# The second block's softmax: scaling by the reciprocal sums moved from a VectorE pass into the transposition on TensorE

## The chip, the cores and the metric

The kernel runs on one core of one Trainium2 chip. The metric is device time in microseconds (us), the median of several runs. A core has TensorE (PE, with its weight loads listed as PEld), VectorE (DVE), ScalarE (ACT), GpSimd (POOL) and the queues that issue transfers. A profile is one execution, recorded instruction by instruction.

## The reference

Two transformer blocks of different make, each of two layers, on 512 tokens of 1024 features, in fp32. The change touches the second block's two kinds of attention. In short:

```
# grouped-query attention: 8 query heads, 2 key heads, 512 keys
s = einsum('bqgrd,bkgd->bgrqk', qi, k) * scale
p = softmax(s, axis=-1)
o = einsum('bgrqk,bkgd->bqgrd', p, v)

# dilated attention: 4 heads, 3 groups of neighbours (steps 1, 4, 16)
s = einsum('bqhd,bqkhd->bhqk', qi, kg) * scale      # masked at the edges
lse = logsumexp(s); p = exp(s - lse)
out_g = einsum('bhqk,bqkhd->bqhd', p, vg)
o = sum over g of softmax over g of (lse_g) * out_g
```

The last line of the dilated attention is the same as one softmax over the keys of all three groups together, and so the kernel does it: 768 columns a query (512 of the first group, 128 each of the others), most of them masked.

## The kernel before

Activations lie with features on the partitions. Each projection is a set of TensorE products in which weights and activations are split in a high and a low part (`split`, `mm3`, lines 121 to 151): three products of 512 columns for each 128 features that are summed over. The weights are loaded, cast on ScalarE (L121) and their low part is made on GpSimd (L122).

`mixers2` runs once in each layer of the second block. It weaves generators: while `gqa` and then `dilated` yield between their steps, `dil_proj` and `gate` issue projections, so that on TensorE their products (L144, L145, L147) stand between the attention's own. A scheduler then fixes the order on each engine, and every engine works its own list in that order.

`gqa` goes over 4 pairs of heads (`u`) and 2 halves of the queries, 8 halves a layer. In a half, for two blocks of 128 queries (`b`) and two heads (`e`): scores in fp32 on TensorE (L1197, from `scores`; 128x512 each), their negated maximum on VectorE (L1221), exponentials with sums on ScalarE (L1225, tile `P`), the reciprocal of the sums (L1227) and a product of `P` with it, in place, both on VectorE (L1229). Then each 128x128 block of `P` is transposed on TensorE (L1237), four of them into one PSUM tile `pt` of two that rotate; ScalarE copies each filled `pt` to SBUF (L1239); the products with the values follow (L1245).

`dilated` does the same with one head at a time and 768 columns: scores L1197 (first pair of heads, 512 and twice 128 columns) or L1200 (second pair), mask and maximum L1268, exponentials L1273, reciprocal L1275, scaling L1276, transpositions L1284, copies L1286, products with the values L1292 and L1298. The first pair of heads runs among the projections of the second, the second among the gates.

A transposition has a block of `P` as its stationary operand and the identity as its moving one:

```
nc.tensor.transpose(pt[:, e, b], P[b][:, e, 128 * kb:128 * kb + 128], self.ident)
```

Of the kernel before, what the change touches and what calls it, by code (L numbers as in the profile page):

```python
# [14 lines left out]
ALU = mybir.AluOpType  # L15
# [74 lines left out]
class Kernel:  # L90
# [1111 lines left out]
    def head_gains(self):  # L1202
# [3 lines left out]
        q = self.hg.rearrange("p (l t g) -> p l t g", l=2, g=4)[:, :, :, 0:2]  # L1206
        nc.vector.tensor_scalar(out=q, in0=q, scalar1=0.125, scalar2=None, op0=ALU.mult)

    def gqa(self, q, k, V, outs):
        nc = self.nc  # L1210
        for u in range(4):
            t = self.new("of", [128, 512], "oa")
            for half in range(2):
                P = []
                for b in range(2):
                    Q = slice(256 * half + 128 * b, 256 * half + 128 * b + 128)
                    ps = self.psum("p2", [128, 2, 512])
                    for e in range(2):
                        self.scores(ps[:, e], q[u], k, e, Q, slice(0, 512))
                    nm = self.new("c1", [128, 2], "nm2")  # L1220
                    nc.vector.tensor_reduce(out=nm, in_=ps, axis=AX.X, op=ALU.max, negate=True)  # L1221
                    p = self.new("P", [128, 2, 512], "P2")
                    z = self.new("c1", [128, 2], "z2")
                    for e in range(2):
                        nc.scalar.activation(out=p[:, e], in_=ps[:, e], func=AF.Exp, bias=nm[:, e:e + 1], accum_out=z[:, e:e + 1])  # L1225
                    rz = self.new("c1", [128, 2], "rz2")
                    nc.vector.reciprocal(out=rz, in_=z)  # L1227
                    for e in range(2):
                        nc.vector.tensor_scalar(out=p[:, e], in0=p[:, e], scalar1=rz[:, e:e + 1], scalar2=None, op0=ALU.mult)  # L1229
                    P.append(p)  # L1230
                yield True
                PT = []
                for kb in range(4):
                    pt = self.psum("pt", [128, 2, 2, 128])
                    for e in range(2):
                        for b in range(2):
                            nc.tensor.transpose(pt[:, e, b], P[b][:, e, 128 * kb:128 * kb + 128], self.ident)  # L1237
                    w = self.new("W", [128, 2, 256], "PT2")
                    nc.scalar.copy(out=w, in_=pt.rearrange("p e b q -> p e (b q)"))  # L1239
                    PT.append(w)  # L1240
                yield True
                acc = self.psum("pt", [128, 256])
                for kb in range(4):
                    for e in range(2):
                        nc.tensor.matmul(acc[64 * e:64 * e + 64], V(0, kb)[:, 64 * e:64 * e + 64], PT[kb][:, e],  # L1245
                                         start=kb == 0, stop=kb == 3, tile_position=(0, 64 * e))
                nc.scalar.copy(out=t[:, 256 * half:256 * half + 256], in_=acc)
                yield True
            outs.append(t)

    def dilated(self, u, q, k, V, outs):

        nc = self.nc
        t = self.new("of", [128, 512], "ob")
        for half in range(2):
            PT = []
            for e in range(2):
                P = []
                for b in range(2):
                    r = 2 * half + b  # L1260
                    Q = slice(128 * r, 128 * r + 128)
                    ps = self.psum("p2", [128, 1024])
                    self.scores(ps[:, 0:512], q[0, u], k[0, u], e, Q, slice(0, 512))
                    for g in (1, 2):
                        self.scores(ps[:, 384 + 128 * g:512 + 128 * g], q[g, u], k[g, u], e, Q, Q)
                    p = self.new("P", [128, 768], "Pd")
                    mx = self.new("c1", [128, 1], "mx")
                    nc.vector.tensor_tensor_reduce(out=p, in0=ps[:, 0:768], in1=self.dmask[:, r], scale=1.0, scalar=-3e38,  # L1268
                                                   op0=ALU.add, op1=ALU.max, accum_out=mx)
                    nm = self.new("c1", [128, 1], "nmd")  # L1270
                    nc.vector.tensor_scalar(out=nm, in0=mx, scalar1=-1.0, scalar2=None, op0=ALU.mult)
                    z = self.new("c1", [128, 1], "zd")
                    nc.scalar.activation(out=p, in_=p, func=AF.Exp, bias=nm, accum_out=z)  # L1273
                    rz = self.new("c1", [128, 1], "rzd")
                    nc.vector.reciprocal(out=rz, in_=z)  # L1275
                    nc.vector.tensor_scalar(out=p, in0=p, scalar1=rz, scalar2=None, op0=ALU.mult)  # L1276
                    P.append(p)
                yield True
                for kp in range(3):
                    pt = self.psum("pt", [128, 2, 2, 128])  # L1280
                    for j in range(2):
                        for b in range(2):
                            c = 256 * kp + 128 * j
                            nc.tensor.transpose(pt[:, j, b], P[b][:, c:c + 128], self.ident)  # L1284
                    w = self.new("W", [128, 2, 256], "PTd")
                    nc.scalar.copy(out=w, in_=pt.rearrange("p j b q -> p j (b q)"))  # L1286
                    PT.append(w)
                yield True
            acc = self.psum("pt", [128, 256])
            for kb in range(4):  # L1290
                for e in range(2):
                    nc.tensor.matmul(acc[64 * e:64 * e + 64], V(1 + u, kb)[:, 64 * e:64 * e + 64], PT[3 * e + kb // 2][:, kb % 2],  # L1292
                                     start=kb == 0, stop=False, tile_position=(0, 64 * e))
            for g in (1, 2):
                for b in range(2):
                    B = slice(128 * b, 128 * b + 128)
                    for e in range(2):
                        nc.tensor.matmul(acc[64 * e:64 * e + 64, B], V(1 + 2 * g + u, 2 * half + b)[:, 64 * e:64 * e + 64],  # L1298
                                         PT[3 * e + 2][:, g - 1, B], start=False, stop=g == 2 and b == 1, tile_position=(0, 64 * e))
            nc.scalar.copy(out=t[:, 256 * half:256 * half + 256], in_=acc)  # L1300
            yield True
        outs.append(t)
# [423 lines left out]
```

## Time and profile before

| | |
|---|---|
| median of 3 runs | 3469.3 us (3465.06 to 3469.94) |
| the profiled execution's own time | 3459.91 us |
| its span, first to last instruction | 3458.1 us |
| mean granted TensorE clock | 0.981 |
| TensorE busy | 3302.1 us, 95% of the span |
| TensorE weight loads | 2627.1 us, 76% |
| VectorE busy | 1722.6 us, 50% |
| ScalarE busy | 1582.0 us, 46% |
| GpSimd busy | 1150.1 us, 33% |

The span is shorter than the time by what lies around the instructions. Busy shares are means over the whole program. Matmuls overlap, one starting before the one before it has ended, so a busy TensorE tells that it had something in flight, and the distance from start to start tells what an instruction costs in a row of its kind.

### The profile page before, as it was taken

The numbers are of one execution on the slowest core, as the hardware profiler recorded it, in microseconds if no ns is written. First come the engines' busy times: TensorE is split into PE (matmuls) and PEld (weight loads), VectorE is DVE, ScalarE is ACT, GpSimd is POOL, SyncE is SP. The second block draws the span as 40 slices with busy tenths as digits, with TensorE's granted clock in tenths as the row PEclk, the third lists the DMA queues.
The fourth block names the chain that finished last, engine by engine and source line by source line (L and its number), as shares of the span: only waits on it lengthen the run. The fifth ranks groups of instructions, "written<-read, shape, count | busy, mean of one in ns | idle before, by whom it ended". The sixth has DMA issues, their size and how long they took to land.

```text
span 3458.1 us, 47235 instructions
## 1 busy us (share of the span) xinstructions
PE 3302.1 (95%) x18518; PEld 2627.1 (76%) x18518; DVE 1722.6 (50%) x2736; ACT 1582.0 (46%) x2824; POOL 1150.1 (33%) x555
## 2 busy tenths in 40 slices
PE   6999998999998899989999999999999999999999
PEld 4666677888887666677888667888888767888887
DVE  5755468343345763564326965564315766462111
ACT  5555445242243554454333666543334666543333
POOL 1222033222235321234443312434444312444443
PEclk8999999999999899999999999999999999999999
DMA  7731134343334321145432101236422101222222
GB/s 275 261 107 55 44 102 142 106 137 113 110 120 156 110 79 42 45 166 191 164 116 102 60 32 58 95 122 211 154 93 91 67 31 54 84 95 90 95 96 97
DMA packets 146705, 377.87 MB, mean 109 GB/s; under 512 B 16737, under 2 KB 32690, under 8 KB 146354
## 3 DMA queue, kind: packets, MB, share of 16 engines
q1 hardware_dynamic: 146482, 374.85, 32.0%
q8 instruction: 146, 2.39, 0.3%
q14 instruction: 77, 0.63, 0.1%
HBM read 363.48 MB, written 9.86 MB: 108 GB/s over the span
## 4 chain that ended last, share of the span: by engine, by line
PE 58%; DVE 8%; ACT 2%; DMA 1%; issue 1%; POOL 0%; SPq 0%; DVEq 0%; ACTq 0%; POOLq 0%
PE pm L144 15%; PE pm L145 15%; PE pm L147 14%; PE p L1197 2%; DVE y L360 1%; DMA g<-in_w_mod 1%; PE pt L1245 1%; PE p L999 1%; PE pm L151 1%; PE pt L1237 1%; PE p L1200 1%; PE pt L145 1%; PE pt L144 1%; PE pt L1284 1%; PE pm L965 1%
## 5 line engine op out<-in xcount | busy, mean ns | idle before, releaser
L122 POOL TENSOR_TENSOR wlo<-raw,whi 128x1024 fp32r<-128x1024 f32 (+2 forms) x461 | 1090.7, 2367 | 2070.6 <-ACT whi L121 1942.8
L121 ACT CAST whi<-raw 128x1024 fp32r<-128x1024 f32 (+2 forms) x468 | 477.0, 1019 | 1065.2 <-PE pm L145 577.9
L144 PE MATMUL pm<-h,whi 128*128 128x512 f32 (+1 forms) x2312 | 855.8, 378 | 15.3 <-ACT raw_s L555 7.3
L145 PE MATMUL pm<-h,whi 128*128 128x512 f32 (+1 forms) x2312 | 842.8, 372 | 1.9 <-DVE h L388 1.9
L147 PE MATMUL pm<-h,wlo 128*128 128x512 f32 x1816 | 716.5, 395 | 2.6 <-POOL wlo L122 2.6
L144 PEld LDWEIGHTS pm<-h,whi 128*128 128x128 f32 x2312 | 441.8, 191 | 101.5 <-issue 10.1
L145 PEld LDWEIGHTS pm<-h,whi 128*128 128x128 f32 x2312 | 441.0, 191 | 78.4 <-issue 6.5
L144 PE MATMUL pm<-hid,whi 128*128 128x512 f32 (+1 forms) x1280 | 457.4, 367 | 4.0 <-DVE x L459 2.2
L145 PE MATMUL pm<-hid,whi 128*128 128x512 f32 (+1 forms) x1280 | 455.2, 365 | 2.9 <-DVE hid L527 2.9
L147 PEld LDWEIGHTS pm<-h,wlo 128*128 128x128 f32 x1816 | 343.3, 189 | 76.7 <-POOL wlo L122 4.3
L147 PE MATMUL pm<-hid,wlo 128*128 128x512 f32 x976 | 381.1, 390 | 0.2 <-POOL wlo L122 0.2
L527 DVE TENSOR_TENSOR hid<-relu,hid 128x512 fp32r<-128x512 f32 (+1 forms) x169 | 177.3, 1053 | 339.0 <-ACT hid L526 338.9
L273 DVE SCALAR_TENSOR_TENSOR p<-g,svec,p 128x512 f32<-128x512 f32 x280 | 211.2, 754 | 258.2 <-DMA g<-in_w_mod 255.3
L459 DVE SCALAR_TENSOR_TENSOR x<-pm,mod,x 128x512 f32<-128x512 f32 (+1 forms) x184 | 125.5, 684 | 383.0 <-PE pm L147 377.4
L144 PEld LDWEIGHTS pm<-hid,whi 128*128 128x128 f32 x1280 | 241.1, 188 | 46.9 <-issue 5.4
L145 PEld LDWEIGHTS pm<-hid,whi 128*128 128x128 f32 x1280 | 240.8, 188 | 41.5 <-DVE hid L527 3.5
L147 PEld LDWEIGHTS pm<-hid,wlo 128*128 128x128 f32 x976 | 183.6, 188 | 39.5 <-POOL wlo L122 1.4
L521 ACT ACTIVATE relu<-pm 128x512 f32<-128x512 f32 (+1 forms) x160 | 85.8, 536 | 130.2 <-PE pm L147 130.2
L978 ACT ACTIVATE D<-pt,cc 128x256 f32<-128x256 f32 (+1 forms) x176 | 72.8, 447 | 81.6 <-PE pt L972 43.3
L339 DVE TENSOR_TENSOR acc<-acc,sq 128x256 f32<-128x256 f32 (+1 forms) x96 | 89.0, 927 | 27.8 <-ACT sq L331 26.3
L523 ACT ACTIVATE relu<-relu 128x512 f32<-128x512 f32 (+1 forms) x169 | 96.3, 570 | 4.8
L387 ACT ACTIVATE h<-y,mod 128x256 fp32r<-128x256 f32 (+1 forms) x136 | 67.0, 527 | 60.1 <-DVE y L360 59.3
(418 smaller groups left out, 4791.3 us busy)
## 6 DMA issues: line engine op xcount, KB each, us to landing
g<-in_w_mod SPq DMA_DIRECT2D x352, 256.0 KB, 3.3
raw<-in_w_in SPq DMA_DIRECT2D x142, 512.0 KB, 3.5
raw<-in_w_down SPq DMA_DIRECT2D x136, 512.0 KB, 3.5
raw<-in_w_up SPq DMA_DIRECT2D x128, 512.0 KB, 3.5
raw<-in_w_out SPq DMA_DIRECT2D x24, 512.0 KB, 3.5
g<-in_w_mod SPq DMA_DIRECT2D x16, 512.0 KB, 7.1
raw<-in_w_out SPq DMA_DIRECT2D x16, 384.0 KB, 3.3
raw<-in_w_br SPq DMA_DIRECT2D x16, 384.0 KB, 3.0
```

Of the source, the lines that this page charges most:

```text
L121: nc.scalar.copy(out=hi, in_=src)
L122: (eng or nc.vector).tensor_tensor(out=lo, in0=src, in1=hi.bitcast(F32), op=ALU.subtract)
L144: nc.tensor.matmul(out, hi[:, k], xh, start=i == 0, stop=False)
L145: nc.tensor.matmul(out, hi[:, k], xl, start=False, stop=False)
L147: nc.tensor.matmul(out, lo[:, k], xh, start=False, stop=i == n - 1)
L273: nc.vector.scalar_tensor_tensor(out=a, in0=g, scalar=sk, in1=a, op0=ALU.mult, op1=ALU.add)
L339: nc.vector.tensor_tensor(out=acc, in0=acc, in1=sq, op=ALU.add)
L459: nc.vector.scalar_tensor_tensor(out=x, in0=ps, scalar=ga[:, m:m + 1], in1=x, op0=ALU.mult, op1=ALU.add)
L521: nc.scalar.activation(out=r, in_=ps, func=AF.Relu)
L523: nc.scalar.activation(out=q, in_=r, func=AF.Square)
L527: nc.vector.tensor_tensor(out=lo, in0=q, in1=hi.bitcast(F32), op=ALU.subtract)
L978: nc.scalar.activation(out=D[:, kk, T], in_=rp[:, kk, T], func=AF.Exp, bias=cc[:, 2 * p + kk, r:r + 1])
```

## The change

The exponentials `P` stay as ScalarE left them. A new function, `diagonal`, takes the reciprocal of the sums and writes, for each column of sums, a 128x128 tile `dg`: the identity times the reciprocals, one for each partition (query). The transposition becomes an ordinary fp32 product with the same stationary block of `P` and `dg` as the moving operand, which transposes the block and scales it by query. `dg` comes from the rotating tiles `W` (16 of them), which also hold the transposed blocks.

```
+    def diagonal(self, z, n):
+
+        nc = self.nc
+        rz = self.new("c1", [128, n], "rz")
+        nc.vector.reciprocal(out=rz, in_=z)
+        dg = self.new("W", [128, n, 128], "dg")
+        for e in range(n):
+            nc.vector.tensor_scalar(out=dg[:, e], in0=self.ident, scalar1=rz[:, e:e + 1], scalar2=None, op0=ALU.mult)
+        return dg
+
     def gqa(self, q, k, V, outs):
...
-                    rz = self.new("c1", [128, 2], "rz2")
-                    nc.vector.reciprocal(out=rz, in_=z)
-                    for e in range(2):
-                        nc.vector.tensor_scalar(out=p[:, e], in0=p[:, e], scalar1=rz[:, e:e + 1], scalar2=None, op0=ALU.mult)
-                    P.append(p)
+                    P.append((p, self.diagonal(z, 2)))
...
-                            nc.tensor.transpose(pt[:, e, b], P[b][:, e, 128 * kb:128 * kb + 128], self.ident)
+                            p, dg = P[b]
+                            nc.tensor.matmul(pt[:, e, b], p[:, e, 128 * kb:128 * kb + 128], dg[:, e], start=True, stop=True)
...
-                    rz = self.new("c1", [128, 1], "rzd")
-                    nc.vector.reciprocal(out=rz, in_=z)
-                    nc.vector.tensor_scalar(out=p, in0=p, scalar1=rz, scalar2=None, op0=ALU.mult)
-                    P.append(p)
+                    P.append((p, self.diagonal(z, 1)))
...
-                            nc.tensor.transpose(pt[:, j, b], P[b][:, c:c + 128], self.ident)
+                            p, dg = P[b]
+                            nc.tensor.matmul(pt[:, j, b], p[:, c:c + 128], dg[:, 0], start=True, stop=True)
```

The scheduler's order changes inside the two attentions of each layer and nowhere else. On VectorE, at the first half of `gqa` in layer 0 (`pt` with `hr`, `hv` and `hraw` is the preparation of other heads, `acc` a norm's sum), before (-) and after (+):

```order
-L1229 TENSOR_SCALAR P_17206<-P_17206,rz_17210 128x512 x2
-L1227 RECIPROCAL rz_17223<-z_17220 128x2
-L162 SCALAR_TENSOR_TENSOR pt<-pt,hr 128x512
-L1229 TENSOR_SCALAR P_17219<-P_17219,rz_17223 128x512 x2
+L1216 TENSOR_SCALAR dg<-ident,rz 128x128 x2
+L1213 RECIPROCAL rz<-z_17221 128x2
+L162 SCALAR_TENSOR_TENSOR pt<-pt,hr 128x512
+L1216 TENSOR_SCALAR dg<-ident,rz 128x128 x2
```

The narrow operations stand where the wide ones stood.

On TensorE, at the end of the seventh half of `gqa` in layer 0, the last transpositions of a half, the products with the values and what follows them, before:

```order
L1237 MATMUL pt<-ident,P_18005 128x128
L1237 MATMUL pt<-ident,P_17992 128x128
L1237 MATMUL pt<-ident,P_18005 128x128
L144 MATMUL pm<-h,whi 128x512
L1245 MATMUL pt<-PT_18018,V_16689 64x256 x2
L1245 MATMUL pt<-PT_18025,V_16689 64x256 x2
L1245 MATMUL pt<-PT_18032,V_16689 64x256 x2
L1245 MATMUL pt<-PT_18039,V_16690 64x256 x2
L1197 MATMUL p_18064<-qk_16869,qk_17074 128x512
L1197 MATMUL p_18064<-qk_16870,qk_17074 128x512
L1237 MATMUL pt<-ident,P_18056 128x128 x2
```

And after, at the same place:

```order
L1244 MATMUL pt<-dg,P_18018 128x128
L1244 MATMUL pt<-dg,P_18004 128x128
L1244 MATMUL pt<-dg,P_18018 128x128
L1252 MATMUL pt<-PT_18032,V_16689 64x256 x2
L1252 MATMUL pt<-PT_18039,V_16689 64x256 x2
L1252 MATMUL pt<-PT_18046,V_16689 64x256 x2
L1252 MATMUL pt<-PT_18053,V_16690 64x256 x2
L1197 MATMUL p_18079<-qk_16869,qk_17074 128x512
L1197 MATMUL p_18079<-qk_16870,qk_17074 128x512
L1244 MATMUL pt<-dg,P_18070 128x128 x2
```

The sequence is the same; one product of a projection (L144) that stood ahead of the products with the values stands elsewhere. A row is one instruction of the program; in the trace an fp32 product is two matmuls with a weight load each, a transposition one.

## Rows read from the trace of the kernel before

**Rows 1.** The page: engines, granted clock in 40 slices, chain that ended last.

```profile
PE 3302.1 (95%) x18518; PEld 2627.1 (76%) x18518; DVE 1722.6 (50%) x2736; ACT 1582.0 (46%) x2824; POOL 1150.1 (33%) x555
...
PEclk8999999999999899999999999999999999999999
...
PE 58%; DVE 8%; ACT 2%; DMA 1%; issue 1%; POOL 0%; SPq 0%; DVEq 0%; ACTq 0%; POOLq 0%
```

**Rows 2.** Windows over both attentions: length, busy time and count by engine, granted clock.

```profile
1916.00:1960.00 44.00, 41.22 (x179) 28.60 (x178) 42.49 (x71) 32.36 (x62) 13.32 (x7) 1.00 0.17 59
1960.00:2047.00 87.00, 85.75 (x435) 56.17 (x437) 56.91 (x101) 51.84 (x111) 14.84 (x7) 1.00 0.12 43
2047.00:2150.00 103.00, 101.64 (x566) 74.57 (x563) 68.54 (x148) 66.35 (x120) 21.77 (x9) 1.00 0.15 51
2715.00:2760.00 45.00, 42.74 (x189) 30.96 (x188) 38.64 (x66) 28.17 (x53) 12.91 (x7) 1.00 0.18 60
2760.00:2837.00 77.00, 75.01 (x392) 47.70 (x391) 52.08 (x95) 50.09 (x110) 12.68 (x7) 1.00 0.10 35
2837.00:2948.00 111.00, 111.00 (x606) 82.65 (x604) 68.70 (x151) 68.49 (x122) 26.93 (x11) 1.00 0.14 50
sum 467.00, PE 457.36 PEld 320.66 DVE 327.36 ACT 297.31 POOL 102.45; mean PE 76.23 PEld 53.44 DVE 54.56 ACT 49.55 POOL 17.07
```

**Rows 3.** Waits of TensorE, 1916 to 2150 us: total, times, longest.

```profile
PE pt L1237 <- DVE P L1229: 3.0, 4, 1.7
PE pt L1245 <- DVE qk L1189: 1.0, 1, 1.0
PE pm L147 <- POOL wlo L122: 0.8, 1, 0.8
PE pt L1284 <- DVE qk L1189: 0.6, 1, 0.6
```

**Rows 4.** The same, 2715 to 2950 us.

```profile
PE pt L1237 <- DVE P L1229: 2.2, 2, 1.4
PE p L1197 <- ACT P L1225: 1.1, 1, 1.1
PE pt L1237 <- DVE qk L1187: 0.8, 1, 0.8
```

**Rows 5.** The transpositions by line: durations (min/median/max ns); idle before them.

```profile
L1237 PEld LDWEIGHTS pt<-ident,P x256: 137/140/146, 1934.2 to 2833.5; 128*128 128x128 f32 x128
L1237 PE MATMUL pt<-ident,P x256: 270/273/333, 1934.2 to 2833.6; 128*128 128x128 f32 x128
...
  ACT PT L1239: 5.3, 22
...
L1284 PE MATMUL pt<-ident,Pd x192: 270/272/329, 2049.1 to 2944.6; 128*128 128x128 f32 x192
...
  ACT PTd L1286: 3.1, 13
```

**Rows 6.** Chain that ended last, 1999 to 2011 us: start, length, what.

```profile
1999.37 0.86 PE p L1197 x2
2000.23 0.87 PE pt L1237 x8
...
2003.29 1.91 PE p L1197 x4
```

**Rows 7.** The fp32 scores by line; the last row from 2030 to 2150 us alone.

```profile
L1197 PEld LDWEIGHTS p<-qk,qk x224: 186/190/246, 1916.4 to 2893.7; 128*128 128x128 f32 x112
L1197 PE MATMUL p<-qk,qk x224: 272/592/697, 1916.6 to 2893.8; 128*128 128x512 f32 x80, 128*128 128x128 f32 x32
...
L1197 PE MATMUL p<-qk,qk x56: 272/275/697, 2030.4 to 2091.8; 128*128 128x128 f32 x32, 128*128 128x512 f32 x24
```

**Rows 8.** Timeline of TensorE, 2039.5 to 2046 us: start, length, line, count.

```profile
2043.17 0.82 PE L1237 MATMUL pt<-ident,P 128*128 128x128 f32 x6
2043.83 0.61 PE L1197 MATMUL p<-qk,qk 128*128 128x128 f32 x4
2044.19 0.48 PE L145 MATMUL pm<-h,whi 128*128 128x512 f32 x1
2044.51 1.03 PE L1237 MATMUL pt<-ident,P 128*128 128x128 f32 x8
```

**Rows 9.** Scaling and reciprocals on VectorE by line.

```profile
L1229 DVE TENSOR_SCALAR P<-P,rz x64: 460/481/2321, 1933.7 to 2831.2; 128x512 f32<-128x512 f32 x64
...
L1276 DVE TENSOR_SCALAR Pd<-Pd,rzd x32: 609/618/952, 2044.0 to 2941.1; 128x768 f32<-128x768 f32 x32
...
L1227 DVE RECIPROCAL rz<-z x32: 144/166/168, 1926.4 to 2830.5; 128x2 f32<-128x2 f32 x32
```

**Rows 10.** VectorE operations of 128 columns elsewhere.

```profile
L925 DVE TENSOR_SCALAR cc<-pt x3: 292/542/545, 71.0 to 1213.2; 128x384 f32<-128x384 f32 x2, 128x128 f32<-128x128 f32 x1
...
L716 DVE COPY V<-pt x56: 273/281/293, 1889.4 to 2904.7; 128x128 f32<-128x128 f32 x56
```

**Rows 11.** ScalarE's copies of the transposed blocks, by line.

```profile
L1239 ACT COPY PT<-pt x64: 575/588/629, 1938.5 to 2834.0; 128x512 f32<-128x512 f32 x64
...
L1286 ACT COPY PTd<-pt x48: 563/587/604, 2051.4 to 2945.6; 128x512 f32<-128x512 f32 x48
```

## The prediction

> **What bounds the kernel now.** I read the page first. TensorE is busy 95% of the span, VectorE 50%, and of the chain that ended last 58% is TensorE and 8% VectorE [rows 1]. But these are means over a long program, and the change touches only the second block's attention, so I cut the span to the six stretches in which it runs: for each layer the start of `gqa`, the rest of it, and `dilated` [rows 2]. The reader should see two things there. In four of the six TensorE is busy for 97% or more, and in the last all of it, at a granted clock of 1.00. In the first, 1916 to 1960 us, VectorE is at 42.49 of 44 us while TensorE is at 41.22. So VectorE paces the start of `gqa` in layer 0, nearly so in layer 1 (38.64 of 45), and from there on the stretches are TensorE's. Over all six, TensorE has nothing in flight for 467.00 - 457.36 = 9.6 us. This is the number on which the forecast turns: whatever VectorE is spared can shorten the kernel by little more than that, and whatever TensorE is given it has to do within stretches that are full.
>
> The waits of TensorE [rows 3, 4] say what the 9.6 us are: 3.0 + 2.2 = 5.2 us are transpositions that wait for the scaling L1229, the rest are waits for prepared heads, for a low part of weights and for exponentials, each once.
>
> **What is removed and added on VectorE.** Removed are 64 scalings of 128x512 at 0.481 us and 32 of 128x768 at 0.618 us: 30.8 + 19.8 = 50.6 us [rows 9]. Added are 96 products of the identity with a column of reciprocals, 128x128. The trace of before has no such form from SBUF in this place. The lower bound is the reciprocal of two columns, 0.166 us [rows 9], which has hardly any data; the upper is the one scaling of 128x128 from PSUM, 0.292 us [rows 10]. Drawing the line through 512 and 768 columns (0.137 us for 256, 0.53 ns a column) down to 128 gives 0.481 - 384 x 0.00053 = 0.28 us, the same as the copies of 128 columns, 0.281 [rows 10]; I take 0.28. 96 x 0.28 = 26.9 us, so VectorE is spared about 24 us (with the bounds, 50.6 - 96 x 0.292 = 22.6 to 50.6 - 96 x 0.166 = 34.7). The reciprocals stay as they are: 32 and 32, before and after.
>
> Most of these 24 us are worth nothing, since TensorE paces. What they are worth lies in the 5.2 us: the chain from sums to the first transposition gets shorter by 2 x (0.481 - 0.28) = 0.40 us in `gqa` and 0.34 in `dilated`. Six waits in all are recorded; six times 0.40 would be 2.4 us. But TensorE also arrives later at each of them, as the next part shows, so I take the whole 5.2 us as gone. The other 4.4 us of idle time I leave standing: they wait for work that this change doesn't shorten. Bounds: 0 to 9.6.
>
> **What is exchanged on TensorE.** 256 transpositions in `gqa` and 192 in `dilated`, 448 in all [rows 5], become fp32 products of the same size with the same stationary block. A transposition in a row of its kind costs the distance from start to start: 8 in 0.87 us, 0.109 us each [rows 6]; the timeline says the same, (1.03 - 0.272) / 7 = 0.108, when the last one's own duration is taken off [rows 5, 8]. It is one matmul with one weight load.
>
> The product is in the trace too, because scores are fp32: `scores` is called for 64 products of 512 columns in `gqa` and 48 (16 of 512, 32 of 128) in `dilated`'s first pair of heads, 112 in all, and the trace has 224 matmuls and 224 weight loads on that line [rows 7]. So an fp32 product is two matmuls. Those of 128 columns have a 128x128 stationary operand and 128 moving columns, just the form that the change makes: four matmuls (two products) in 0.61 us [rows 8], the last lasting 0.275 (the median where these are the most) [rows 7], thus (0.61 - 0.275) / 3 = 0.112 us from start to start. A product is 2 x 0.112 = 0.223 us where the transposition is 0.109, and 448 x 0.114 = 51.1 us more for TensorE. A matmul of 512 columns in the same fp32 path takes 0.86 / 2 = 0.43 us [rows 6], four times 0.11, so in this path columns set the time, and the 128 columns of a transposition are bound by something else, its weight load most likely; that is why the ratio is two and not more.
>
> Here a rule of the Trainium skill speaks against the change more strongly than the row. "TensorE: Matmul & The Clock Gate", section Terms, says that the transpose mode of weight loads and matmuls is four times faster for FP32. By it each transposition turned into a product would cost three times 0.109 us more, 448 x 0.327 = 146 us in all. The rows of this kernel show 0.223 against 0.109, a factor of 2.05, with both kinds of 128 columns side by side in one microsecond [rows 8]; the sum goes by them.
>
> Is any of the 51.1 us hidden? In `gqa` the transposed blocks leave in groups of four, copied by ScalarE in 0.588 us [rows 11], and two such PSUM tiles rotate. Four transpositions take 0.436 us, four products 0.89. If the copies paced the groups now, the first 0.15 us of each group's extra would be hidden: 112 groups (64 and 48 copies) x 0.152 = 17.0 us. But weight loads that waited for these copies make up only 5.3 + 3.1 = 8.4 us [rows 5], the waits of the matmuls themselves show none of it [rows 3, 4], and a row of eight transpositions, two full tiles, runs at 0.109 us throughout. So I take 0, with 8.4 us as the bound.
>
> The new tile `dg` takes a place among 16 rotating tiles; a half of `gqa` uses 2 + 4 of them, one of `dilated` 10, and by the time a place comes round its old content was read by products that are over. I cost it at nothing; if a place were late, VectorE would wait at `dg`, the preparation of heads (L162 to L189) is queued behind it, and TensorE's products behind those. Nothing else moves: the order differs only inside the two attentions, and no transfer is issued elsewhere.
>
> **The sum.** 51.1 - 5.2 = +45.9 us, 1.3%. Against the profiled execution's own 3459.91 us this is 3505.8; its span is 1.8 us shorter. The median of the runs lies 9.4 us above the profiled execution, and the changed kernel's runs should lie as much above theirs, so I forecast 3469.3 + 45.9 = 3515 us. A difference of 0.2%, 7 us, is about what a measurement of this kernel can tell from none.
>
> **The rivals.**
> *More of it is hidden.* All idle time, 9.6 us, and all that waited for copies, 8.4, take up products: 51.1 - 18.0 = +33.1, 3502 us. For it: TensorE, loaded more, finds everything else ready earlier. Against: some idle time is a single wait for heads or weights. Chance 0.15, for results between this and the forecast's own range.
> *VectorE is the bound after all (the other side).* If the softmax chain on VectorE paced all six stretches as it does 1916 to 1960 us, the products would hide behind it and the saving would show: 3469.3 - 24 = 3445 us. It decides once TensorE idles for at least 51 us in them; it idles for 9.6. Chance 0.03, with another 0.02 for a result near no change.
> *The order turns against it.* The scheduler has shuffled projections and attention products, and a `dg` can be late as scalings were: one L1229 took 2.321 us instead of 0.481 [rows 9]. If none of the idle time is won and half a dozen more such delays of 1.8 us reach TensorE, it is 51.1 + 11 = +62, 3531 us. Chance 0.08.
> *Transpositions are four times faster,* as the page has it: +146 us, 3616 us. Chance 0.03.
>
> The forecast has what is left, 0.69, with its own range from 3507 to 3522: the whole idle time won, or none of it and a few microseconds of run to run (the three runs span 4.9 us). To leave out no more than 2 in 10, the range reaches to the first rival, less some of that spread, and part of the way to the third: 3499 to 3526. Faster 0.03, same 0.02, slower 0.95.
>
> **What would show it.** In the changed kernel's trace: 896 matmuls on the two lines of the products, 0.11 us from start to start, weight loads near 0.190 us instead of 0.140; operations on `dg` of 0.28 us; the six stretches together longer by about 46 us, TensorE busy in nearly all of it, waits for `dg` below 2 us; all other stretches as before. I am wrong if products come at another pace than the scores of 128 columns, or if the stretches before held slack that busy time doesn't show.

## The result

The changed kernel takes 3510.4 us, median of 4 runs (3503.15 to 3512.39), against 3469.4 us of the kernel before (4 runs, 3465.06 to 3469.94). The ratio is 1.0127, 95% interval 1.0108 to 1.0146: slower by 44 us, between 37 and 51 (the two medians differ by 41.0). The forecast was 3515 us, slower by 46.

### The profile after

The profiled execution took 3509.29 us, its span is 3507.5 us. The lines of its page that answer to [rows 1]:

```profile
PE 3350.3 (96%) x18966; PEld 2680.7 (76%) x18966; DVE 1694.5 (48%) x2736; ACT 1584.7 (45%) x2824; POOL 1148.1 (33%) x555
...
PEclk9999999999999899999999999999999999999999
...
PE 56%; DVE 8%; DMA 2%; ACT 2%; issue 1%; POOL 0%; SPq 0%; DVEq 0%; ACTq 0%; POOLq 0%
```

TensorE has exactly 448 matmuls more (18966 - 18518), VectorE as many operations as before and 28 us less of them. The page alone doesn't say where the time went; windows do. Both traces are cut at the first score and at the last product with the values of each layer's attention. First the kernel before (start and end, length, busy time and count of TensorE, its weight loads, VectorE, ScalarE and GpSimd, then the granted clock):

```profile
0.00:1916.60 1916.60, 1788.97 (x11120) 1425.02 (x11121) 986.42 (x1579) 846.01 (x1580) 591.14 (x313) 0.97 0.37 124
1916.60:2146.10 229.50, 224.10 (x1155) 155.62 (x1154) 166.69 (x317) 148.95 (x288) 49.93 (x23) 1.00 0.14 49
2146.10:2722.00 575.90, 565.24 (x2770) 471.42 (x2771) 258.10 (x359) 246.59 (x391) 242.47 (x105) 0.99 0.35 122
2722.00:2948.10 226.10, 221.85 (x1153) 155.55 (x1151) 153.25 (x300) 142.02 (x276) 49.88 (x23) 1.00 0.13 47
2948.10:3458.10 510.00, 501.89 (x2327) 419.44 (x2325) 158.11 (x183) 198.39 (x291) 216.72 (x91) 0.99 0.27 94
```

Then the changed one:

```profile
0.00:1917.30 1917.30, 1787.44 (x11120) 1421.00 (x11121) 986.73 (x1579) 845.80 (x1580) 590.91 (x313) 0.97 0.37 124
1917.30:2169.10 251.80, 247.48 (x1373) 183.30 (x1372) 151.97 (x317) 150.06 (x288) 49.33 (x23) 1.00 0.13 45
2169.10:2747.00 577.90, 566.97 (x2776) 472.61 (x2776) 258.67 (x359) 246.55 (x391) 242.35 (x105) 0.99 0.36 121
2747.00:2996.70 249.70, 245.60 (x1371) 183.50 (x1369) 139.26 (x300) 144.03 (x276) 49.23 (x23) 1.00 0.13 43
2996.70:3507.50 510.80, 502.86 (x2331) 420.26 (x2331) 157.87 (x183) 198.26 (x291) 216.27 (x91) 0.99 0.27 93
```

The two attention stretches grew from 229.5 + 226.1 = 455.6 us to 251.8 + 249.7 = 501.5 us, by 45.9. All else grew by 3.5 us, and 2.8 of these are the attention's doing too: 224 matmuls were added in each layer, but only 218 more are counted in each stretch (1373 - 1155, 1371 - 1153), because six projection products that stood inside it now come behind its end, at 0.23 us from start to start. With them the cost is 48.7 us.

Inside the stretches VectorE has 319.9 - 291.2 = 28.7 us less to do, and TensorE's idle time (length less busy time) is 9.65 us before and 8.42 after. So VectorE's saving bought at most 1.2 us of TensorE's idle time.

The products with `dg` in `gqa` (L1244), the weight loads of those in `dilated` (L1289), and the diagonal (L1216); durations are min/median/max in ns:

```profile
L1244 PE MATMUL pt<-dg,P x512: 270/275/377, 1934.7 to 2872.9; 128*128 128x128 f32 x171
...
L1289 PEld LDWEIGHTS pt<-dg,Pd x384: 186/192/192, 2061.5 to 2993.5; 128*128 128x128 f32 x192
...
L1216 DVE TENSOR_SCALAR dg<-ident,rz x96: 264/281/2375, 1934.4 to 2990.0; 128x128 f32<-128x128 f32 x96
```

And TensorE's timeline in `gqa` of layer 0 (start, length, line, count):

```profile
2018.81 1.50 PE L1244 MATMUL pt<-dg,P 128*128 128x128 f32 x12
2020.15 1.02 PE L1197 MATMUL p<-qk,qk 128*128 128x512 f32 x2
2021.01 1.95 PE L1244 MATMUL pt<-dg,P 128*128 128x128 f32 x16
```

512 + 384 = 896 matmuls; sixteen in a row take 1.95 us, (1.95 - 0.275) / 15 = 0.112 us each, where eight transpositions took 0.87 us [rows 6]: twice the matmuls, each a little dearer. The diagonal's 0.281 us is what was drawn from the wider rows, but its longest is 2.375 us, as long as the longest scaling [rows 9].

TensorE's waits, which answer to [rows 3, 4] (total, times, longest); first layer 0, then layer 1:

```profile
PE pt L1244 <- DVE dg L1216: 2.8, 3, 1.6
PE pt L1252 <- DVE qk L1189: 1.2, 1, 1.2
PE pt L1289 <- DVE qk L1189: 0.2, 1, 0.2
...
PE p L1197 <- ACT P L1235: 1.4, 1, 1.4
PE pt L1244 <- DVE dg L1216: 1.3, 1, 1.3
PE pt L1244 <- DVE qk L1187: 0.7, 1, 0.7
PE pt L1252 <- ACT PT L1246: 0.5, 1, 0.5
```

The diagonal is waited for 4.1 us where the scaling was for 5.2.

### The profile page after: what moved, and what is told of

Read it like the earlier page. It is cut to its first block, busy times and chain, and to the rows that moved or that the text cites. A ratio compares the mean times of both kernels' runs of the same rounds, so it can differ in the third digit from the quotient of the medians.

```text
span 3507.5 us, 48158 instructions
## 1 busy us (share of the span) xinstructions
PE 3350.3 (96%) x18966; PEld 2680.7 (76%) x18966; DVE 1694.5 (48%) x2736; ACT 1584.7 (45%) x2824; POOL 1148.1 (33%) x555
## 4 chain that ended last, share of the span: by engine, by line
PE 56%; DVE 8%; DMA 2%; ACT 2%; issue 1%; POOL 0%; SPq 0%; DVEq 0%; ACTq 0%; POOLq 0%
PE pm L144 14%; PE pm L145 14%; PE pm L147 13%; DMA g<-in_w_mod 2%; PE p L1197 2%; PE pt L1244 2%; PE pt L1289 1%; DVE y L360 1%; PE pt L1252 1%; PE p L999 1%; PE pm L151 1%; PE p L1200 1%; PE pt L144 1%; PE pt L145 1%; PE pm L965 1%
## 5 line engine op out<-in xcount | busy, mean ns | idle before, releaser
L122 POOL TENSOR_TENSOR wlo<-raw,whi 128x1024 fp32r<-128x1024 f32 (+2 forms) x461 | 1088.8, 2363 | 2126.8 <-ACT whi L121 1967.7
L144 PE MATMUL pm<-h,whi 128*128 128x512 f32 (+1 forms) x2312 | 852.9, 377 | 15.1 <-ACT raw_s L555 7.1
L144 PEld LDWEIGHTS pm<-h,whi 128*128 128x128 f32 x2312 | 438.9, 190 | 103.2 <-issue 12.4
L144 PE MATMUL pm<-hid,whi 128*128 128x512 f32 (+1 forms) x1280 | 457.4, 367 | 4.4 <-DVE x L459 2.6
L144 PEld LDWEIGHTS pm<-hid,whi 128*128 128x128 f32 x1280 | 241.1, 188 | 47.5 <-issue 6.9
```

The lines of the kernel that those rows point to most:

```text
L122: (eng or nc.vector).tensor_tensor(out=lo, in0=src, in1=hi.bitcast(F32), op=ALU.subtract)
L144: nc.tensor.matmul(out, hi[:, k], xh, start=i == 0, stop=False)
```

## The experiments

The question was which part of the 44 us belongs to the products and which to everything else that the change does: VectorE's relief, the new tile with its waits, the new order. In the table "time" is from the ratio of each run to the kernel before, with its 95% interval, taken of 3469 us; "stretches" is the length of both attention stretches in the one profiled execution of each, against 455.6 us before.

| run | time against before, us | stretches, us |
|---|---|---|
| changed kernel | +44 (37 to 51) | +45.9 |
| products with the identity, scaling kept | +51 (45 to 58) | +49.4 |
| no scaling, transpositions kept | -7 (-10 to -4) | -5.4 |
| change in `gqa` alone | +25 (19 to 31) | +26.5 |
| change in `dilated` alone | +20 (14 to 26) | +17.7 |
| `gqa` alone, rounded products | +19 (14 to 24) | +16.9 |
| scaling reads PSUM (`gqa`) | +26 (19 to 32) | +30.5 |
| scaling on ScalarE (`gqa`) | 0 (-4 to +3) | -0.2 |
| diagonal of ones, transpositions | +9 (5 to 12) | +7.1 |
| every transposition twice | +58 (52 to 62) | +53.0 |
| diagonal on ScalarE | +49 (43 to 55) | +46.3 |

Two things in the last column are not the edit's own work. First, the projection products that moved behind the stretches: add 2.8 us for the changed kernel (48.7), the products with the identity (52.2), `dilated` alone (20.5) and every transposition twice (55.8), and 2.3 for the diagonal on ScalarE (48.6); in the other runs none moved. Second, TensorE's granted clock. It is 1.00 (2.4 GHz) throughout the stretches of the kernel before and of the changed one, but in six other traces it was 0.50 (1.2 GHz) for a part of them, each time after waits of TensorE: for 3.4 us in all with the products alone and with the diagonal on ScalarE, 6.8 us with the rounded products, with the diagonal of ones and with every transposition twice, 23.9 us with the scaling from PSUM. At half the clock no more than half of such a time is lost, so up to 1.7, 3.4 and 12.0 us of those rows are the clock's. Each trace is one execution; whether the clock fell in the other runs too isn't shown.

### The products alone

```
-nc.tensor.transpose(pt[:, e, b], P[b][...], self.ident)
+nc.tensor.matmul(pt[:, e, b], P[b][...], self.ident, start=True, stop=True)
```

and the same in `dilated`.

> The scaling stays on VectorE as before; only the 448 transpositions become fp32 products with the identity. Theory (TensorE's second matmul is the whole cost, VectorE's relief is worth next to nothing): about as slow as the changed kernel, +48 to +53 us, with 896 matmuls 0.112 us apart; TensorE's idle time in the attention stretches 7 to 10 us as before. Rival (VectorE's relief of some 24 us pays part of the products): 60 us or more, since this kernel has the products without the relief. Rival (the new tile and its waits or the new order cost the time, not the products): under +25 us.

Ratio 1.0148 (1.0129 to 1.0167), +51 us. The stretches of its trace:

```profile
1919.60:2174.50 254.90, 248.22 (x1373) 184.54 (x1371) 167.88 (x317) 150.31 (x288) 49.51 (x23) 0.99 0.14 44
...
2752.40:3002.50 250.10, 245.68 (x1371) 183.95 (x1370) 154.16 (x300) 143.76 (x276) 49.80 (x23) 1.00 0.13 42
```

254.9 + 250.1 = 505.0 us, 49.4 more than before, with VectorE as busy as before. The products alone account for the whole loss; the 60 us or more of the first rival lie above the interval (45 to 58). By the runs the rest of the change gives back 7 us, but the two intervals overlap; by the stretches 3.5 us, of which up to 1.7 are the clock (0.50 from 1970.9 to 1974.2 us). TensorE's idle time is 11.1 us here, above the 7 to 10 expected; 8.3 us of its waits are for the scaling.

### No scaling

The 96 scalings L1229 and L1276 are taken out, the transpositions stay.

> Leaves out the scaling by the reciprocal sums (64 + 32 VectorE operations, 50.6 us of them), transpositions as before; the output lacks that factor. It bounds what any relief of VectorE here can give. Theory (TensorE paces the attention): 0 to -6 us, no more than the idle time that waited for the scaling, 5.2 us. Rival (VectorE paces): -20 us or more.

Ratio 0.998 (0.997 to 0.9989), -7 us (-10 to -4), 450.2 us in the stretches, 5.4 less than before. Taking 50.6 us from VectorE is worth 7 us: these stretches are not VectorE's. The stretches lost about the 5.2 us that were recorded as waits for the scaling, and leaving the scaling out altogether is the most that any relief of VectorE from it can bring.

### One attention at a time

`gqa` as changed with `dilated` as before, and the reverse.

> The change in gqa alone, dilated as before. Theory: 256 x 0.114 = 29.2 us less 1 or 2 us of idle time won, +26 to +30 us. With the dilated part alone it adds up to the whole change. Rival (the cost comes from few places where the diagonal is late): out of proportion to 256 of 448.

> The change in dilated alone, gqa as before. Theory: 192 x 0.114 = 21.9 us and nothing won, since TensorE has no idle time there: +19 to +23 us. Rival (VectorE's relief is used in these stretches, 32 x 0.34 us): +11 us or less.

Ratios 1.0072 (1.0055 to 1.0089) and 1.0057 (1.004 to 1.0075): +25 and +20 us. They add up to 45, the whole change, and stand as 256 to 192 products would: 0.098 and 0.103 us a product. The first is a microsecond below what was expected, well within its interval. The cost is not in a few places. The trace of the second is 17.7 us longer in the stretches, 20.5 with the projection products that moved out of them.

### Every transposition twice

Each `nc.tensor.transpose` line stands twice, the second writing the same place.

> The kernel before with every transposition done twice into the same place: 896 matmuls with a weight load each, as many as the products have, at 0.109 us. Theory (the attention stretches are full, an added matmul costs its distance to the next): +45 to +50 us, as much as the kernel with products instead of transpositions and the scaling kept. Rival (those stretches hide some of it, and fp32 itself costs more than a second matmul): under +35 us.

Ratio 1.0166 (1.0151 to 1.018), +58 us (52 to 62), above the 45 to 50 expected. No fp32 product is in it, only the added matmuls with their weight loads:

```profile
L1237 PE MATMUL pt<-ident,P x256: 270/273/421, 1939.7 to 2888.6; 128*128 128x128 f32 x128
...
L1238 PE MATMUL pt<-ident,P x256: 271/273/421, 1939.9 to 2888.8; 128*128 128x128 f32 x128
```

These are the two lines in `gqa`. The second row is the added line; it lasts as long as the first. 448 x 0.109 = 48.8 us were added, and the stretches grew by 55.8 with what moved out of them. Of the 7 us between, up to 3.4 are the clock (0.50 from 2062.2 to 2069.0 us), and TensorE's idle time is 12.1 us instead of 9.65. So an added transposition costs its distance to the next here, as an added matmul of an fp32 product does; none of it was hidden.

### The change without the second matmul

```
-nc.vector.reciprocal(out=rz, in_=z)
+nc.vector.tensor_scalar(out=rz, in0=z, scalar1=0.0, scalar2=1.0, op0=ALU.mult, op1=ALU.add)
...
-nc.tensor.matmul(pt[:, e, b], p[...], dg[:, e], start=True, stop=True)
+nc.tensor.transpose(pt[:, e, b], p[...], dg[:, e])
```

> The whole change but for the second matmul: the diagonal is made with ones in place of the reciprocals, by operations of the same number and size, and serves as the identity of a transposition, which waits for it as the product did. Leaves out the scaling by the reciprocal sums. Theory (the second matmul is the cost, the run with rounded products lost its time to something of its own): -2 to -8 us against before, much like the run without any scaling. Rival (the waits for the diagonal and the new order cost some 15 us, as the run with rounded products might say): +8 us or more.

Ratio 1.0026 (1.0015 to 1.0036), +9 us: not the -2 to -8 of the theory, but its rival's side. TensorE's waits in both layers:

```profile
PE pt L1244 <- DVE dg L1216: 5.6, 5, 1.9
PE pt L1173 <- DVE qk L1187: 1.9, 1, 1.9
...
PE pt L1244 <- DVE dg L1216: 3.1, 2, 1.9
```

And the stretches:

```profile
1920.60:2154.70 234.10, 225.61 (x1155) 157.55 (x1153) 158.71 (x317) 147.77 (x288) 49.76 (x23) 0.99 0.15 47
2730.50:2959.10 228.60, 223.18 (x1153) 157.14 (x1151) 140.26 (x300) 141.85 (x276) 49.14 (x23) 0.99 0.15 47
```

Here the narrow diagonal is waited for 8.7 us, more than the wide scaling in the kernel before (5.2 us), and the stretches grow by 7.1: 4.3 us of idle time, and 2.8 us of busy time for as many matmuls, which the clock can account for. So the diagonal by itself brings no gain here. The two parts don't add: 7.1 us for the diagonal with transpositions, 49.4 for products with the scaling, 45.9 for both.

That the products of the changed kernel cover these waits, so that 4.1 us remain, is not what the traces show. In each kernel some of the 96 scalings or diagonals are held up while GpSimd works (the part on the waits at the scaling, below, shows how), and how many are, and for how long, differs from kernel to kernel. Added up over their line's median they are 12.6 us late with the diagonal of ones, of which TensorE waits for 8.7; 13.4 us with the products alone, 8.3 waited for; 8.4 us in the changed kernel, 4.1 waited for; 8.9 us before, 5.2 waited for. The 4.6 us between 8.7 and 4.1 thus go with 4.2 us by which the diagonals themselves are later. The scheduler's order isn't the same in these two kernels; what moves the operations beside GpSimd's instruction or away from it wasn't tested.

### Rounded products

```
-dg = self.new("W", [128, n, 128], "dg")
+dg = self.new("W", [128, n, 128], "dg", F32R)
...
-p = self.new("P", [128, 2, 512], "P2")
+p = self.new("P", [128, 2, 512], "P2", F32R)
```

> The change in gqa alone, as in the run that had only that, with the exponentials and the diagonal written in the rounded fp32r type, so that a product is one matmul; the order on every engine is the same as in that run. It rounds the weights of the attention. Theory (the second matmul is the cost): the 128-column matmul comes every 0.11 us like a transposition, so +25 us go to between -5 and +2 us against the kernel before. Rival (the waits for the diagonal or the new order cost it): stays above +15 us.

Ratio 1.0055 (1.0041 to 1.007), +19 us, where -5 to +2 were expected. The line and the stretches:

```profile
L1244 PE MATMUL pt<-dg,P x256: 220/275/626, 1935.3 to 2849.7; 128*128 128x128 f32 x128
...
1917.90:2153.40 235.50, 227.90 (x1155) 159.23 (x1153) 158.00 (x317) 149.25 (x288) 50.22 (x23) 0.99 0.14 47
2730.20:2967.20 237.00, 225.27 (x1153) 159.29 (x1152) 147.90 (x300) 142.31 (x276) 49.80 (x23) 0.99 0.14 44
```

256 matmuls instead of 512, as meant, and yet only 6 us less than with fp32 products in the same order. Of the 16.9 us that the stretches are longer than before, 9.7 are idle time of TensorE (472.5 - 453.2 = 19.3 us against 9.65): in layer 1, 3.8 us for copies of transposed blocks and 3.7 for the diagonal. With the fp32 products of the run with `gqa` alone the idle time is 8.2 us, so slower products hide these waits in this order. The other 7.2 us are busy time. Up to 3.4 of it are the clock, which was 0.50 from 1939.3 to 1942.6 and from 2854.1 to 2857.4 us; the rest stays open. A halved matmul count is worth its time only when what it covered is not waited for instead.

### Where the waits at the scaling come from

In the trace of the kernel before, nine of the 96 scalings started while GpSimd's L122 was running. These nine, and no others, were held up, by 0.3 to 1.8 us, and each ended 0.28 to 0.42 us after L122. In the changed kernel it is eight of the 96 diagonals, which end 0.08 to 0.09 us after it. One place of the changed kernel, GpSimd and then VectorE on the timeline:

```profile
1988.48 2.38 POOL L122 TENSOR_TENSOR wlo<-raw,whi 128x1024 fp32r<-128x1024 f32 x1 [2.04 <-ACT whi L121]
...
1989.92 1.22 DVE L1216 TENSOR_SCALAR dg<-ident,rz 128x128 f32<-128x128 f32 x2
```

L122 ends at 1990.86; the first of the two diagonals, of 128 columns, starts at 1989.92 and lasts until 1990.95. It stands until GpSimd is done, and its end follows L122's, however early it started. "SBUF — State Buffer" of the Trainium skill, section Who interferes with whom, has the rule: VectorE in a two-port mode, which `tensor_scalar` can enter, and GpSimd exclude one another, and whichever issues first keeps the ports for its whole instruction. The trace agrees in this order, GpSimd first; that VectorE was in such a mode no row can show. By the rule a narrower operation waits as long as a wide one, which is what the diagonal did (2.375 us against 2.321).

Three ways round it were run. The scaling that reads PSUM:

```
-nc.scalar.activation(out=p[:, e], in_=ps[:, e], func=AF.Exp, ...)
+nc.scalar.activation(out=ps[:, e], in_=ps[:, e], func=AF.Exp, ...)
...
-nc.vector.tensor_scalar(out=p[:, e], in0=p[:, e], scalar1=rz[:, e:e + 1], ...)
+nc.vector.tensor_scalar(out=p[:, e], in0=ps[:, e], scalar1=rz[:, e:e + 1], ...)
```

> The kernel before, but in gqa the exponentials stay in the scores' PSUM tile and the scaling reads them there and writes P to SBUF. If TensorE's waits for the scaling come from scalings held up beside GpSimd's L122 (0.481 us becoming up to 2.3), a reader of PSUM should escape them: no scaling over 1 us, waits for it below 3 us, and the time -4 to 0 us against before, though each then takes some 0.69 us. If they come from VectorE's queue, or the scores' tiles are now held too long: 0 to +10 us.

Ratio 1.0075 (1.0056 to 1.0093), +26 us, beyond both sides of the expectation. The scaling by line, TensorE's longest wait in layer 0, and the stretches:

```profile
L1229 DVE TENSOR_SCALAR P<-p,rz x64: 729/743/757, 1932.2 to 2865.5; 128x512 f32<-128x512 f32 x64
...
PE pt L1237 <- DVE P L1229: 20.3, 8, 3.9
...
1917.70:2177.90 260.20, 235.34 (x1155) 159.43 (x1153) 173.96 (x317) 150.04 (x288) 49.38 (x23) 0.96 0.13 42
2754.30:2980.20 225.90, 222.25 (x1153) 156.67 (x1152) 159.05 (x300) 142.82 (x276) 49.67 (x23) 0.99 0.15 46
```

None of the 64 is held up any more, though 14 of them started while L122 ran; four scalings of `dilated` (L1276, still from SBUF) that started so in this run were all held, for up to 2.462 us. So that half of the expectation holds. The time is lost all the same, and all of it in layer 0: TensorE waits there for the scaling 20.3 us, while layer 1, with the same edit, is as long as before. Each scaling is 0.26 us longer, and it holds the scores' tile: VectorE's maximum L1221 waited 40.1 us for scores instead of 23.7. But the order changed too: in layer 0 the last three halves of `gqa` have no projection product on TensorE (17, 13 and 8 before) and last 17 us each. There the granted clock is 0.83 over 60 us (2017.7 to 2077.7), in which TensorE is busy for 40. What the longer scaling alone would cost isn't shown.

The scaling on ScalarE (`nc.scalar.activation(..., func=AF.Copy, scale=rz[:, e:e + 1])` in place of L1229):

> The kernel before, but gqa's 64 scalings run on ScalarE, which is busy for 52 of 87 us there. Relief of VectorE by 31 us without any more work for TensorE. Without any scaling at all the gain was 7 us, so at most -5 us; if ScalarE's copies of the transposed blocks queue behind the scalings: 0 to +15 us.

Ratio 0.9999 (0.9989 to 1.0009), no change: the waits for the scaling went to 0.7 us over both layers, and others took their place, 2.4 us for prepared heads (L1187) and 1.2 for a norm's sum in layer 0.

The diagonal of the changed kernel on ScalarE:

```
-nc.vector.tensor_scalar(out=dg[:, e], in0=self.ident, scalar1=rz[:, e:e + 1], scalar2=None, op0=ALU.mult)
+nc.scalar.activation(out=dg[:, e], in_=self.ident, func=AF.Copy, scale=rz[:, e:e + 1])
```

> The changed kernel with the diagonal made on ScalarE (96 operations of 128x128) instead of VectorE. In the traces every diagonal and every scaling that starts while GpSimd's L122 runs ends only after it. Theory (that, not VectorE's own work, is what TensorE waits for at the diagonal): none of the 96 takes over 0.6 us, TensorE's recorded waits for the diagonal fall from 4.1 us to under 1.5, and the time is +36 to +41 us against before, up to 5 us under the changed kernel. Rival (the waits come from the place in an engine's queue): the waits stay or move to the ScalarE operation, +41 us or more.

Ratio 1.0141 (1.0124 to 1.0158), +49 us (43 to 55), where 36 to 41 were expected. The diagonal by line, and TensorE's longest wait in layer 0:

```profile
L1216 ACT ACTIVATE dg<-ident,rz x96: 384/401/451, 1932.6 to 2994.1; 128x128 f32<-128x128 f32 x96
...
PE pt L1252 <- DVE qk L1189: 3.7, 1, 3.7
```

No diagonal is late, though 13 started while L122 ran, and no matmul waits for one, as expected; the time isn't won. One wait of 3.7 us for prepared heads stands in place of the 4.1. GpSimd's hold is thus what delays the scaling and the diagonal, but with either of them on ScalarE TensorE's wait moved to the next operation that VectorE owes it. No version that computes the whole result beat the kernel before.

## Why the prediction was right

**What bounds it.** Right. Without the scaling at all the kernel gains 7 us of the 50.6 us taken from VectorE, and added matmuls cost their full distance. Even layer 0, at whose start VectorE was read as the pace, is only 0.8 us shorter without it (228.7 us), layer 1 4.6 (221.5 us).

**The products.** 448 x 0.114 = 51.1 us was the term. In the changed kernel's trace the cost with what moved out of the stretches is 48.7 us, and the idle time is 1.2 us less, so the products took 49.9 us, 0.111 each; the run with the products alone gives 51 us (45 to 58). The scores of 128 columns were the right row to price them by: 0.112 us a matmul, two a product, weight loads 0.192 us. The factor of four that the Trainium skill gives the transpose mode ("TensorE: Matmul & The Clock Gate", Terms) is not what this kernel shows at 128 columns: 0.223 against 0.109 us. That a transposition's weight load sets its 0.109 us is a guess of the prediction that no run tested.

**VectorE's saving.** The operations on `dg` take 0.281 us at the median, 0.28 was drawn. The lengths of the scalings less those of the operations on `dg` add up to 24.0 us, as forecast, held ones included on both sides; the other 4.7 of the 28.7 us are other VectorE operations that came out shorter.

**The 5.2 us.** This term was mis-sized. I took TensorE's waits for the scaling as gone, because the chain would be 0.40 us shorter each time and TensorE would arrive later. But idle time fell by 1.2 us only. 4.1 of the 5.2 us stayed, as waits for the diagonal, where I expected less than 2: they come from operations that are held until GpSimd is done, whatever their width.

**The sum.** Forecast were 51.1 - 5.2 = 45.9 us; the trace has 49.9 - 1.2 = 48.7. I also took the runs to lie 9.4 us above the profiled execution, as before; the changed kernel's median lies 1.2 us above its own. The runs give 44 us with an interval from 37 to 51, which can't tell these sums apart, so that 46 came within 2 us of 44 is luck. That the products are the cost and VectorE's work is worth almost nothing is not luck: the runs show it.

**Nothing else moves.** Not quite: six projection products a layer, which stood among the attention's, come behind its end in the changed kernel, and 2.8 us with them.

**Hidden by the copies.** Taken as 0. Products of 49.9 us instead of 51.1 leave little to hide, and every transposition twice lost more than its matmuls.

**The rivals.** That more is hidden (+33, 3502 us) lies below the interval of the runs. VectorE as the bound is excluded by the run without scaling, transpositions four times faster by 44 us instead of 146. Late diagonals are real: the run with the diagonal of ones loses 9 us (5 to 12) where 2 to 8 were to be won. In the changed kernel the idle time still fell by 1.2 us, so they didn't turn the sum.

## What to carry to other kernels

Before work is moved from an engine with room to one that is full, price it on the full one by a row of the same form: here an fp32 product of 128 columns costs two matmuls where a transposition costs one, and 50 us of VectorE's work were worth 7. A wait for an operation is not shortened by a narrower one when what it waits for is another engine's instruction; look at what runs beside the longest of its kind, not at its median. And the parts of a change, run one by one, need not add up to the whole: each run can have its own order, its own operations that meet another engine's instruction, and its own stretches at the lower clock. Look for these in the traces before a difference of a few microseconds is put down to the edit.

## What the runs showed of the hardware

A VectorE `tensor_scalar` from SBUF to SBUF that started while GpSimd's L122, a `tensor_tensor`, was running ended only after it: nine of nine before, eight of eight in the changed kernel, up to 2.375 us for an operation of 0.281. The same operation reading PSUM was never held (14 started so, longest 0.757 us), nor was ScalarE (13 started so, longest 0.451 us).

A product in the rounded type (fp32r) of 128 columns in a row of its kind comes every 0.11 us (median 0.112), no faster than one matmul of an fp32 product (0.112) or a transposition (0.109).

TensorE's granted clock fell to 0.50 (1.2 GHz) inside these stretches only in runs in which TensorE had waited just before, and in the worst case stood at 0.83 over 60 us in which TensorE was busy for 40. Waits can thus cost more than their own length; but similar waits in the changed kernel (1.6 us for the diagonal in layer 0) passed without such a fall, so no rule is drawn from this.
